# Twelve weight chunks per layer through GpSimd DMAs, from four pairs of buffers, in a two-layer streaming encoder

## The chip, the cores and the metric

The kernel runs on one core of one Trainium2 chip. The metric is the device time of one execution in microseconds; lower is better. The engines are called PE (TensorE), PEld (its weight load), DVE (VectorE), ACT (ScalarE), POOL (GpSimd) and SP (SyncE, which here only issues DMAs).

## The reference

A sequence of 512 positions of width 1024 passes through two layers. Each layer is a half-step SwiGLU feed-forward block, a mixer, and a second half-step feed-forward block, all with RMS norm and a shift, a scale and a gate that come from a vector c. All data and weights are float32. The mixer, cut to what matters here:

```python
proj = h @ w_in                       # q, k, v of branch A; u of B; q, k, v of C; forget logits; gates
ya = chunked_relpos_attention(qa, ka, va, ..., rel_bias)          # 8 heads of 64, own chunk and 8 before
yb = multiscale_pool(ub, w_pool, pool_scale)
yc = forgetting_attention(qc, kc, vc, ..., f_lin + forget_bias)   # 8 heads of 64, causal, decaying bias
branch = einsum('bsnw,nwd->bsnd', stack([ya, yb, yc]), w_branch)
merged = sum(sigmoid(g_lin) * branch, over the 3 branches)
return merged @ w_out
```

## The kernel before

**Products.** A float32 weight or activation is held as two parts of the format fp32r: a high part (`hi`) and the remainder (`lo`). `triple` forms each product from three matmuls: hi x hi (L119), lo x hi (L120, here the weight's low part, written `acc<-wlo,hhi`) and hi x lo (L121). `hhi` and `hlo` are the two parts of the normed activations.

**Weight chunks.** `wchunk` (L237 to 265) fetches 512 KB of float32 weights by a DMA that SP issues into a tile of the tag `raw`, which has two buffers (`NRAW` = 2). ACT casts it to the high part `whi` (L262), and `lo_eng` subtracts that from the raw values to give `wlo` (L264). `whi` and `wlo` have three buffers each. `lo_eng` is DVE, except between the start of the attention of branch A and the end of that of branch C, where `LO_SHARE` = 1 gives every subtraction to POOL.

**The stage around the change.** The weights of q, k, v of branch A are columns 0, 1, 2 of `w_qkv`, those of branch C columns 3, 4, 5; each column is four chunks. `proj` streams chunks 0 and 1 of a column past all four row tiles; chunks 2 and 3 are `held`, and used row tile by row tile, so that each row tile is finished in turn. `Mixer.run` first drains columns 0 to 2. Then `attention(..., "a")` runs the eight heads of branch A, and between its steps takes matmuls from a filler: `fill_a` is columns 3, 4, 5 and then the forget gates (`forget`). The attention of branch C follows, with the gates and branch products (`merge_units`, from weight chunks `w_branch` and `w_ubg`) as its filler. In the profile, the filler's columns of layer 0 run from 471 to 576 us, those of layer 1 from 1716 to 1821 us.

**The order.** Program order gives each tile and its buffer; `later` and `poll` place the transposes and value products of a head among the filler's matmuls by a count of PE work (`pe`). A tile scheduler then lays each engine's instructions in one fixed order. An engine takes its queue strictly in that order, and waits at an instruction whose inputs or whose target buffer are not ready; a DMA waits in the queue of the engine that issues it.

**Steps of the attention that come up later.** L765 and L766: logits (two matmuls). L769: bias and maximum on DVE. L773: exponential on ACT. L776: division by the row sum, as a `tensor_scalar` on DVE. L788: transposes on PE. L792 and L793: high and low part of the transposed probabilities (`pta`, `ptb`), on ACT and DVE. L810 and L811: value products. L814, L815, L369, L370: output of a head and its split. L270 to L278: Newton steps for the inverse norms of q and k (`nt_v`, `nt_j`, `nt_q`, `nt_u`, `nt_z`) on DVE; L653: their application, on DVE and POOL. L712, L713, L716: forget logits. L196, `v<-in_w_ada_dram`: the weight loads of the modulation, elsewhere in the program.

Of the kernel before, what the change touches and what calls it, by code (L numbers as in the profile page):

```python
# [22 lines left out]
P = 128  # L23
T = 512
# [16 lines left out]
def encoder_kernel(tc, xT, c, w_ada, b_ada, gains, w_gate, w_up, w_down, w_qkv, w_f, w_ubg,  # L41
# [22 lines left out]
    def st(shape, dt, tag, bufs):  # L64
        return sb.tile(shape, dt, tag=tag, bufs=bufs, name=nm(tag))
# [171 lines left out]
    def wchunk(src, shape, side=True, spare=None, lo_eng=None):  # L237
        if lo_eng is None:
            lo_share[1] += 1
            lo_eng = nc.gpsimd if lo_share[0] and lo_share[1] % lo_share[0] == 0 else nc.vector  # L240
        if quiet[0] > 0:
            quiet[0] -= 1
            if quiet[0] == 0:
                gate.clear()
        elif side and in_ffn[0] and mod_tag[0] == "v2":
            mod_credit[0] += MOD_RATE
            while mod_credit[0] >= 1.0:
                mod_credit[0] -= 1.0
                mod_pop()
        raw = st([P] + list(shape), F32, "raw", NRAW)  # L250
        last["dma"] = nc.sync.dma_start(raw, src).ins
        if spare == "ptb":
            both = st([P, 2] + list(shape), F32R, "ptb", 2)
            hi, lo = both[:, 0], both[:, 1]
        elif spare == "b":
            hi = st([P] + list(shape), F32R, "b", NB)
            lo = st([P] + list(shape), F32R, "b", NB)
        else:
            hi = st([P] + list(shape), F32R, "whi", 3)
            lo = st([P] + list(shape), F32R, "wlo", 3)  # L260
        with behind("scalar"):
            nc.scalar.copy(hi, raw)  # L262
        with behind("vector"):
            lo_eng.tensor_tensor(lo, raw, hi.bitcast(F32), op=ALU.subtract)  # L264
        return hi, lo


    def rsqrt(v, n):
# [307 lines left out]
            return [self.act(n, *pgs[n]) for n in range(3)]  # L576


    def qkv_chunk(l, col, c, **kw):
        return wchunk(w_qkv[l, 2 * c * P:(2 * c + 2) * P, col * T:(col + 1) * T]  # L580
                      .rearrange("(k p) c -> p k c", p=P), (2, T), **kw)

    def proj(l, col, evac, pre=None, norm=None):
        accs = [acc() for _ in range(NT)]

        def three(t, k, hi, lo):
            tk = slice(t * P, (t + 1) * P)
            triple2(accs[t], hhi[:, k, tk], hlo[:, k, tk], hi, lo, k == 0, k == KD - 1)

        if norm is not None:  # L590
            for hs in range(2):
                norm.back(hs, mmt)
                if hs == 0:
                    later(FRONT2, lambda: norm.front(1, mmt))
                    later(BACK2, lambda: norm.back(1, mmt))
                for k in range(6):
                    hi, lo = pre[k // 2]
                    for t in (2 * hs, 2 * hs + 1):
                        three(t, k, hi[:, k % 2, :], lo[:, k % 2, :])
        else:  # L600
            for c in range(2):
                hi, lo = qkv_chunk(l, col, c)
                for kk in range(2):
                    for t in range(NT):
                        three(t, 2 * c + kk, hi[:, kk, :], lo[:, kk, :])
                        yield
        held = [(c, *qkv_chunk(l, col, c)) for c in ((3,) if pre else (2, 3))]
        for t in range(NT):
            for c, hi, lo in held:
                for kk in range(2):  # L610
                    three(t, 2 * c + kk, hi[:, kk, :], lo[:, kk, :])
                    yield
            evac(t, accs[t])
# [1 line left out]
    def triple2(o, lh, ll, rh, rl, start, stop):  # L615
        triple(o, lh, ll, rh, rl, start, stop)

    def proj_v(l, col, tag, res):
        vt = [None] * NT

        def evac(t, a):
            b = st([P, H, 2, HD], F32R, tag, 4)
            a3 = a.rearrange("p (h d) -> p h d", h=H)
            for odd in range(2):
                hi, lo = b[:, odd::2, odd, :], b[:, odd::2, 1 - odd, :]
                split_to(hi, lo, a3[:, odd::2, :])
            vt[t] = b

        yield from proj(l, col, evac)
        res.extend(vt)  # L630

    def proj_qk(l, col, gcol, is_q, res, pre=None, norm=None):
# [70 lines left out]
    def forget(l):  # L703
        raw = st([P, KD, H], F32, "wf", 1)
        nc.sync.dma_start(raw, w_f[l])
        f2 = st([P, KD, 40], F32R, "ssum", 1)
        nc.gpsimd.memset(f2.bitcast(F32), 0.0)
        split_to(f2[:, :, :H], f2[:, :, 32:32 + H], raw)
        pf = mmt()
        for k in range(KD):  # L710
            poll()
            mm(pf[:40, :], f2[:, k, :], hhi[:, k, :], start=(k == 0), stop=False)  # L712
            mm(pf[:40, :], f2[:, k, :], hlo[:, k, :], start=False, stop=(k == KD - 1))  # L713
            pe[0] += 2.0
        z = t1(T)[:H, :]
        nc.scalar.copy(z, pf[32:32 + H, :])  # L716
# [196 lines left out]
    def drain(*gens):  # L913
        for it in gens:
            for _ in it:
                pass

    class Mixer:
# [10 lines left out]
        def run(self, nxt):  # L929
            l = self.l  # L930
            in_ffn[0] = False
            for b in range(4):
# [2 lines left out]
            g8 = qg8[:, l, :]  # L935
            qa, ka, va, qc, kc, vc = [], [], [], [], [], []
            ya, yb, yc = [], [], []
            drain(proj_qk(l, 0, g8[:, 0:1], True, qa, self.pre, self.norm),
                  proj_qk(l, 1, g[:, 1:2], False, ka), proj_v(l, 2, "xv", va))
            finish_turns()  # L940
            turns.clear()
            heads[0] = 0

            def fill_a():
                yield from proj_qk(l, 3, g8[:, 2:3], True, qc)
                yield from proj_qk(l, 4, g[:, 3:4], False, kc)
                yield from proj_v(l, 5, "v2", vc)
                yield from forget(l)

            lo_share[0] = LO_SHARE  # L950
# [134 lines left out]
```

## Time and profile before

| what | value |
|---|---|
| three runs | 2504.58, 2512.98, 2509.06 us |
| median | 2509.06 us |
| the profiled execution, its own time | 2514.29 us |
| its span in the profile | 2512.5 us |
| granted PE clock, mean over the span | 0.995 |
| weight chunks through `wchunk` | 395 casts on ACT, of which 24 are the change's |

The span is what the hardware profiler recorded from the first to the last instruction; every row below is from that one execution. In a row of a timeline the columns are start, duration, engine, line, operation and output<-inputs; the square bracket at its end is the engine's idle time before it and what ended that. A row of groups gives count, busy time, mean in ns, then the idle time before the group's instructions. In a row on DMA issues the last figure is the median time from issue to landing.

### The profile page before, as it was taken

The numbers are of one execution on the slowest core, as the hardware profiler recorded it, in microseconds if no ns is written. First come the engines' busy times: TensorE is split into PE (matmuls) and PEld (weight loads), VectorE is DVE, ScalarE is ACT, GpSimd is POOL, SyncE is SP. The second block draws the span as 40 slices with busy tenths as digits, with TensorE's granted clock in tenths as the row PEclk, the third lists the DMA queues.
The fourth block names the chain that finished last, engine by engine and source line by source line (L and its number), as shares of the span: only waits on it lengthen the run. The fifth ranks groups of instructions, "written<-read, shape, count | busy, mean of one in ns | idle before, by whom it ended". The sixth has DMA issues, their size and how long they took to land. (4 is left out here: it accounts for less than half of the span.)

```text
span 2512.5 us, 30820 instructions
## 1 busy us (share of the span) xinstructions
PE 2440.8 (97%) x11898; PEld 2039.0 (81%) x11898; DVE 1374.1 (55%) x2429; ACT 979.7 (39%) x1632; POOL 384.8 (15%) x369
## 2 busy tenths in 40 slices
PE   6999999999999999999999999999899999999999
PEld 5888888777788888888888888877778888888888
DVE  8655536688753365555365543367787434533332
ACT  4322235767532343222332223355766334422231
POOL 2000003243322220000020000123332322100000
PEclk9999999999999999999999999999999999999999
DMA  7655533222323335555335532323233233222322
GB/s 252 227 188 198 191 111 110 76 80 91 107 89 109 119 113 196 185 201 184 101 117 187 192 121 97 118 84 93 64 110 102 92 116 121 74 95 98 97 96 93
DMA packets 116263, 320.02 MB, mean 127 GB/s; under 512 B 11122, under 2 KB 13298, under 8 KB 116116
## 3 DMA queue, kind: packets, MB, share of 16 engines
q1 hardware_dynamic: 116114, 318.05, 37.6%
q8 instruction: 93, 1.52, 0.2%
q14 instruction: 54, 0.44, 0.1%
q10 hardware_dynamic: 2, 0.00, 0.0%
HBM read 311.64 MB, written 6.38 MB: 127 GB/s over the span
## 5 line engine op out<-in xcount | busy, mean ns | idle before, releaser
L262 ACT CAST whi<-raw 128x1024 fp32r<-128x1024 f32 (+1 forms) x395 | 411.7, 1045 | 1096.9 <-PE acc L120 421.5
L264 DVE TENSOR_TENSOR wlo<-raw,whi 128x1024 fp32r<-128x1024 f32 x339 | 419.0, 1238 | 532.2 <-ACT whi L262 520.1
L120 PE MATMUL mm<-hlo,whi 128*128 128x512 f32 x1304 | 507.8, 389 | 0.0
L121 PE MATMUL mm<-hhi,wlo 128*128 128x512 f32 x1304 | 507.7, 389 | 0.0
L119 PE MATMUL mm<-hhi,whi 128*128 128x512 f32 x1304 | 507.6, 389 | 0.0
L119 PE MATMUL acc<-b,whi 128*128 128x512 f32 (+1 forms) x960 | 359.0, 374 | 0.0
L121 PE MATMUL acc<-b,wlo 128*128 128x512 f32 (+1 forms) x960 | 357.2, 372 | 0.0
L120 PE MATMUL acc<-b,whi 128*128 128x512 f32 (+1 forms) x960 | 356.6, 372 | 0.0
L121 PEld LDWEIGHTS mm<-hhi,wlo 128*128 128x128 f32 x1304 | 245.0, 188 | 51.0
L119 PEld LDWEIGHTS mm<-hhi,whi 128*128 128x128 f32 x1304 | 245.0, 188 | 51.0
L120 PEld LDWEIGHTS mm<-hlo,whi 128*128 128x128 f32 x1304 | 245.0, 188 | 50.7
L309 POOL TENSOR_TENSOR ssum<-ssum,t 128x256 f32<-128x256 f32 (+1 forms) x45 | 53.6, 1190 | 1082.4 <-ACT t L308 1082.4
L121 PEld LDWEIGHTS acc<-b,wlo 128*128 128x128 f32 x960 | 184.6, 192 | 29.8
L120 PEld LDWEIGHTS acc<-b,whi 128*128 128x128 f32 x960 | 184.5, 192 | 29.1 <-DVE b L370 0.3
L119 PEld LDWEIGHTS acc<-b,whi 128*128 128x128 f32 x960 | 184.6, 192 | 28.9
L196 DVE CUSTOM_DVE_ANT_0 v<-v,b,badac 128x1024 f32<-128x1024 f32 x144 | 183.8, 1279 | 35.5 <-DMA v<-in_w_ada_dram 35.4
L119 PE MATMUL acc<-hhi,whi 128*128 128x512 f32 x480 | 192.0, 401 | 3.2 <-ACT hhi L555 3.2
L121 PE MATMUL acc<-hhi,wlo 128*128 128x512 f32 x480 | 190.1, 396 | 3.3 <-POOL wlo L264 3.1
L120 PE MATMUL acc<-hlo,whi 128*128 128x512 f32 x480 | 189.4, 395 | 1.5 <-DVE hlo L557 1.5
L454 DVE TENSOR_TENSOR t<-mm,t 128x512 f32<-128x512 f32 x86 | 59.4, 691 | 212.7 <-PE mm L121 208.6
L264 POOL TENSOR_TENSOR wlo<-raw,whi 128x1024 fp32r<-128x1024 f32 (+1 forms) x56 | 133.6, 2389 | 175.3 <-ACT whi L262 145.8
L119 PE MATMUL acc<-whi,hhi 128*128 128x512 f32 x336 | 138.2, 411 | 4.9 <-ACT t L642 3.7
(233 smaller groups left out, 3552.9 us busy)
## 6 DMA issues: line engine op xcount, KB each, us to landing
v<-in_w_ada_dram SPq DMA_DIRECT2D x144, 512.0 KB, 4.4
raw<-in_w_down_dram SPq DMA_DIRECT2D x88, 512.0 KB, 3.7
raw<-in_w_gate_dram SPq DMA_DIRECT2D x85, 512.0 KB, 3.4
raw<-in_w_up_dram SPq DMA_DIRECT2D x85, 512.0 KB, 3.4
raw<-in_w_ubg_dram SPq DMA_DIRECT2D x56, 512.0 KB, 3.5
raw<-in_w_qkv_dram SPq DMA_DIRECT2D x48, 512.0 KB, 3.7
raw<-in_w_branch_dram SPq DMA_DIRECT2D x24, 512.0 KB, 3.7
raw<-in_w_out_dram SPq DMA_DIRECT2D x16, 512.0 KB, 3.7
```

The source lines that it names most:

```text
L119: mm(o, lh, rh, start=start, stop=False)
L120: mm(o, lh, rl, start=False, stop=False)
L121: mm(o, ll, rh, start=False, stop=stop)
L196: nc.vector.tensor_tensor_reduce(out=raw, in0=raw, in1=silc[0], scale=1.0, scalar=badac[:, l, j, d:d + 1], op0=ALU.mult, op1=ALU.add, accu ...
L262: nc.scalar.copy(hi, raw)
L264: lo_eng.tensor_tensor(lo, raw, hi.bitcast(F32), op=ALU.subtract)
L309: nc.gpsimd.tensor_tensor(self.ssum[:, cols], self.ssum[:, cols], q, op=ALU.add)
L454: nc.vector.tensor_tensor(pr, pu, sg, op=ALU.mult)
```

## The change

The 12 chunks of columns 3, 4 and 5 no longer go through `wchunk`. A `Stream` makes both parts of each: `begin` lets a DMA issued by GpSimd convert the float32 weights to fp32r on their way into `hi`; `end` lets ACT write the negated high part into `lo` and a second DMA of GpSimd add the same weights of the DRAM onto it, which leaves the remainder. `get`, called where a chunk is wanted, begins chunks up to two ahead (`AHEAD` = 2) and ends them up to one ahead. Chunk 0 is begun and ended while column 2 is being computed (`early`, called behind the request of that column's held chunks). Every fourth chunk takes the two `raw` buffers as its pair, so that there are four pairs with the three of `whi` and `wlo`. The matmuls are the same.

```diff
+    class Stream:
+        AHEAD = 2
...
+        def early(self):
+            self.begin()
+            self.end()
+
+        def begin(self):
+            n = self.begun
+            self.begun += 1
+            if n % 4 == 3:
+                hi, lo = (st([P] + self.shape, F32R, "raw", NRAW) for _ in range(2))
+            else:
+                hi, lo = st([P] + self.shape, F32R, "whi", 3), st([P] + self.shape, F32R, "wlo", 3)
+            nc.gpsimd.dma_start(hi, self.chunks[n])
+            self.parts.append((hi, lo))
+
+        def end(self):
+            hi, lo = self.parts[self.ended]
+            nc.scalar.activation(lo, hi.bitcast(F32), AF.Copy, scale=-1.0)
+            nc.gpsimd.dma_start(lo, self.chunks[self.ended], accum_op=ALU.add)
+            self.ended += 1
+
+        def get(self):
+            n = self.at
+            self.at += 1
+            while self.begun < len(self.chunks) and self.begun <= n + self.AHEAD:
+                self.begin()
+            while self.ended < self.begun and self.ended <= n + 1:
+                self.end()
+            return self.parts[n]
...
     def qkv_chunk(l, col, c, **kw):
-        return wchunk(w_qkv[l, 2 * c * P:(2 * c + 2) * P, col * T:(col + 1) * T]
-                      .rearrange("(k p) c -> p k c", p=P), (2, T), **kw)
+        if stream[0] is not None:
+            return stream[0].get()
+        return wchunk(qkv_src(l, col, c), (2, T), **kw)
...
         held = [(c, *qkv_chunk(l, col, c)) for c in ((3,) if pre else (2, 3))]
+        if held_hook is not None:
+            held_hook()
...
+            coming = Stream([qkv_src(l, col, c) for col in (3, 4, 5) for c in range(4)], [2, T])
             drain(proj_qk(l, 0, g8[:, 0:1], True, qa, self.pre, self.norm),
-                  proj_qk(l, 1, g[:, 1:2], False, ka), proj_v(l, 2, "xv", va))
+                  proj_qk(l, 1, g[:, 1:2], False, ka), proj_v(l, 2, "xv", va, coming.early))
...
             def fill_a():
+                stream[0] = coming
                 yield from proj_qk(l, 3, g8[:, 2:3], True, qc)
                 yield from proj_qk(l, 4, g[:, 3:4], False, kc)
                 yield from proj_v(l, 5, "v2", vc)
+                stream[0] = None
                 yield from forget(l)
```

In the changed file the new class is L267 to 304: the high part's DMA is L288, the negation L293, the accumulating DMA L294. What stood at L653 stands at L700 there, L739 is L786, L765 and L766 are L812 and L813, L788 is L835. In the fences that follow, a number behind a tile's name tells the tiles of one tag apart.

POOL's queue in layer 0, at the start of the stage, before (`ptb` is the k of branch A being normalised):

```order
L653 TENSOR_TENSOR ptb_528_3228<-ptb_528_3228,nt_z_553_3345 128x512 x2
L264 TENSOR_TENSOR wlo_595_3559<-raw_593_3556,whi_594_3558 128x1024
L264 TENSOR_TENSOR wlo_612_3618<-raw_610_3615,whi_611_3617 128x1024
L264 TENSOR_TENSOR wlo_634_3698<-raw_632_3695,whi_633_3697 128x1024
L264 TENSOR_TENSOR wlo_637_3704<-raw_635_3701,whi_636_3703 128x1024
L740 MEMSET strip_671_3850 64x64
```

And after. Chunk 0 is `whi_570` and `wlo_571`, chunk 1 `whi_595` and `wlo_596`, chunk 2 `whi_597` and `wlo_598`, chunk 3 the pair of raw buffers, `raw_613` (high) and `raw_614` (low):

```order
L288 DMA raw_613_3622<-in_w_qkv_dram 128x2x512
L700 TENSOR_TENSOR ptb_528_3228<-ptb_528_3228,nt_z_553_3345 128x512 x2
L288 DMA whi_570_3429<-in_w_qkv_dram 128x2x512
L294 DMA raw_614_3623<-in_w_qkv_dram 128x2x512
L294 DMA wlo_571_3430<-in_w_qkv_dram 128x2x512
L288 DMA whi_595_3561<-in_w_qkv_dram 128x2x512
L288 DMA whi_597_3564<-in_w_qkv_dram 128x2x512
L294 DMA wlo_596_3562<-in_w_qkv_dram 128x2x512
L294 DMA wlo_598_3565<-in_w_qkv_dram 128x2x512
L288 DMA whi_634_3701<-in_w_qkv_dram 128x2x512
```

In place of each subtraction two DMAs now stand in POOL's queue, and chunk 3 goes ahead of chunk 0.

PE's queue where chunk 1 is first used, before (row tile by row tile, three matmuls each):

```order
L766 MATMUL mm_604_3603<-b_571_3440,b_527_3213 128x384
L119 MATMUL acc_589_3552<-whi_611_3617,hhi_114 128x512
L120 MATMUL acc_589_3552<-wlo_612_3618,hhi_114 128x512
L121 MATMUL acc_589_3552<-whi_611_3617,hlo_115 128x512
L119 MATMUL acc_590_3553<-whi_611_3617,hhi_114 128x512
L120 MATMUL acc_590_3553<-wlo_612_3618,hhi_114 128x512
```

After, in layer 0:

```order
L813 MATMUL mm_607_3610<-b_573_3445,b_527_3213 128x384
L119 MATMUL acc_591_3557<-whi_595_3561,hhi_114 128x512
L119 MATMUL acc_592_3558<-whi_595_3561,hhi_114 128x512
L119 MATMUL acc_593_3559<-whi_595_3561,hhi_114 128x512
L119 MATMUL acc_594_3560<-whi_595_3561,hhi_114 128x512
L835 MATMUL mm_615_3639<-ident_66,t2_602_3587 128x128 x2
L812 MATMUL mm_616_3644<-b_573_3445,b_526_3212 128x512
L120 MATMUL acc_591_3557<-wlo_596_3562,hhi_114 128x512
L121 MATMUL acc_591_3557<-whi_595_3561,hlo_115 128x512
```

Four L119, the transposes and a logit product now stand ahead of the first L120, which reads chunk 1's low part. Elsewhere in the stage PE's order is the one of before.

SP's queue at the end of the stage of layer 0, before:

```order
L251 DMA raw_862_4514<-in_w_qkv_dram 128x2x512
L251 DMA raw_971_4886<-in_w_branch_dram 128x2x512
L739 DMA strip_891_4631<-in_rel_dram 128x512
L251 DMA raw_974_4892<-in_w_ubg_dram 128x1024
L251 DMA raw_1016_5058<-in_w_ubg_dram 128x1024
L251 DMA raw_1074_5264<-in_w_branch_dram 128x2x512
```

And after:

```order
L786 DMA strip_839_4451<-in_rel_dram 128x512
L786 DMA strip_879_4619<-in_rel_dram 128x512
L251 DMA raw_959_4874<-in_w_branch_dram 128x2x512
L251 DMA raw_962_4880<-in_w_ubg_dram 128x1024
L251 DMA raw_1004_5046<-in_w_ubg_dram 128x1024
L251 DMA raw_1062_5252<-in_w_branch_dram 128x2x512
```

The column's loads are gone from SP. The first two loads of the next stage, `raw_959` and `raw_962`, take the two buffers that chunk 11, the last of the stream and again a fourth one, has filled with its high and low part.

More of the change, by code (lines that the diff above doesn't have):

```diff
@@ L265, in wchunk, with __init__ @@
         return hi, lo
+    class Stream:
+        AHEAD = 2
+        def __init__(self, chunks, shape):
+            self.chunks, self.shape = chunks, shape
+            self.begun, self.ended, self.at = 0, 0, 0
+            self.parts = []
+        def early(self):
[23 more added lines that the diff above has]
+            return self.parts[n]
     def rsqrt(v, n):
@@ L576, in start, with qkv_src, proj @@
             return [self.act(n, *pgs[n]) for n in range(3)]
+    stream = [None]
+    def qkv_src(l, col, c):
+        return w_qkv[l, 2 * c * P:(2 * c + 2) * P, col * T:(col + 1) * T].rearrange("(k p) c -> p k c", p=P)
     def qkv_chunk(l, col, c, **kw):
-        return wchunk(w_qkv[l, 2 * c * P:(2 * c + 2) * P, col * T:(col + 1) * T]
-                      .rearrange("(k p) c -> p k c", p=P), (2, T), **kw)
-    def proj(l, col, evac, pre=None, norm=None):
+        if stream[0] is not None:
+            return stream[0].get()
+        return wchunk(qkv_src(l, col, c), (2, T), **kw)
+    def proj(l, col, evac, pre=None, norm=None, held_hook=None):
         accs = [acc() for _ in range(NT)]
@@ L616, in triple2, with proj_v @@
         triple(o, lh, ll, rh, rl, start, stop)
-    def proj_v(l, col, tag, res):
+    def proj_v(l, col, tag, res, held_hook=None):
         vt = [None] * NT
@@ L627, in evac @@
             vt[t] = b
-        yield from proj(l, col, evac)
+        yield from proj(l, col, evac, held_hook=held_hook)
         res.extend(vt)
```

## The prediction

> **What bounds the kernel now.** I read the page's busy table first, then a table of the two stages that the change touches, then PE's waits in them.
>
> ```profile
> span 2512.5 us, 30820 instructions
> PE 2440.8 (97%) x11898; PEld 2039.0 (81%) x11898; DVE 1374.1 (55%) x2429; ACT 979.7 (39%) x1632; POOL 384.8 (15%) x369
> ```
>
> PE is busy 97% of the span, and the change neither adds nor removes a matmul. So time can move only through PE's waits and its clock. In the stretch of columns 3 to 5 (layer 0, then layer 1; the columns are length, then busy time and count of PE, PE's loads, DVE, ACT, POOL, then clock, DMA share and rate):
>
> ```profile
> 471.00:576.00 105.00, 98.19 (x504) 79.37 (x503) 80.53 (x209) 72.41 (x160) 40.91 (x30) 0.98 0.24 73
> 1716.00:1821.00 105.00, 96.64 (x504) 77.97 (x503) 80.69 (x209) 72.45 (x160) 41.29 (x30) 1.00 0.24 73
> ```
>
> PE lacks 6.8 us of the 105 in layer 0 and 8.4 us in layer 1. DVE at 77% is the next engine; ACT stands at 69%, POOL at 39%, the DMA engines at 24%. What PE waits for, from 471 to 590 us (total, times, longest):
>
> ```profile
> PE mm L765 <- DVE t L815: 1.6, 2, 1.1
> PE mm L788 <- DVE nt_z L278: 1.2, 1, 1.2
> ...
> PE mm L811 <- DVE ptb L793: 0.8, 1, 0.8
> ...
> PE mm L810 <- ACT pta L792: 0.2, 1, 0.2
> ```
>
> Twelve rows, 7.6 us together, nearly all on DVE, and not one names a weight part (whi or wlo) or its DMA: the weights are on time now. Whatever the change does for their transport brings nothing by itself. It can bring time only by freeing DVE, and it can cost time by making a weight late.
>
> **What goes.** Per layer the change removes 12 casts on ACT, 12 subtractions on POOL and 12 loads of SP:
>
> ```profile
> L264 POOL TENSOR_TENSOR wlo<-raw,whi 128x1024 fp32r<-128x1024 f32 x14 | 33.7, 2412 | 56.1 <-ACT whi L262 43.0 <-PE acc L119 8.8 <-issue 4.2
> L262 ACT CAST whi<-raw 128x1024 fp32r<-128x1024 f32 x15 | 15.7, 1049 | 2.2 <-PE acc L121 2.0
> L653 POOL TENSOR_TENSOR ptb<-ptb,nt_z 128x512 f32<-128x512 f32 x4 | 6.0, 1518 | 7.3 <-DVE nt_z L278 7.3
> raw<-in_w_qkv_dram SPq DMA_DIRECT2D x9, 512.0 KB, 3.6
> ```
>
> Off POOL go 12 x 2.41 = 28.9 us. On ACT a negation of the same shape stands for each cast; I price it at the cast's 1.05 us, so nothing changes there in sum. Why POOL's passes matter:
>
> ```profile
> 542.12 4.76 POOL L264 TENSOR_TENSOR wlo<-raw,whi 128x1024 fp32r<-128x1024 f32 x2 [8.85 <-PE acc L119]
> 544.60 2.32 DVE L270 TENSOR_SCALAR nt_j<-nt_v 128x32 int32<-128x32 int32 x1
> 506.01 0.18 DVE L270 TENSOR_SCALAR nt_j<-nt_v 128x32 int32<-128x32 int32 x1
> 541.19 0.28 DVE L776 TENSOR_SCALAR t<-t,rs 128x128 f32<-128x128 f32 x1
> 487.40 2.03 DVE L776 TENSOR_SCALAR t<-t,rs 128x128 f32<-128x128 f32 x1
> ```
>
> The same small DVE operation lasts 0.18 us alone and 2.32 us when it meets a POOL subtraction; the one of L776 0.28 and 2.03 us. It holds DVE for about as long as POOL's pass lasts. The page "SBUF — State Buffer" of the Trainium skill (section "Who interferes with whom") describes this as an exclusive lock on a port that DVE and GpSimd share, and the rows above agree.
>
> This block at 544.60 ends in a PE wait, and in something worse:
>
> ```profile
> 547.84 0.52 PE L788 MATMUL mm<-ident,t 128*128 128x128 f32 x3 [1.21 <-DVE nt_z L278]
> 545.00:549.00 4.00, 2.52 (x13) 1.51 (x11) 3.87 (x10) 0.69 (x2) 1.88 (x1) 1.00 0.62 177
> 549.00:553.00 4.00, 4.00 (x13) 3.39 (x14) 3.83 (x11) 2.32 (x5) 2.05 (x2) 0.57 0.43 151
> 1798.93 0.66 PE L788 MATMUL mm<-ident,t 128*128 128x128 f32 x4 [1.70 <-DVE t L776]
> 503.62 2.36 DVE L648 TENSOR_SCALAR nt_v<-qss 128x32 f32<-128x32 f32 x1
> 507.30 0.39 PE L811 MATMUL mm<-ptb,xv 128*128 128x256 f32 x1 [0.83 <-DVE ptb L793]
> 548.99 0.44 PE L811 MATMUL mm<-pta,xv 128*128 128x256 f32 x1 [0.23 <-DVE pta L793]
> ```
>
> After the 1.21 us gap the granted clock falls from 1.00 to a mean of 0.57 over four us: (1 - 0.57) x 4 = 1.7 us of work lost. Layer 1 has its gap at the same place (1.70 us) without such a fall.
>
> Gain, layer 0: the waits of 1.2 and 0.8 us (the second at 507.3, with a blocked operation of DVE 1.3 us ahead of it), 0.2 for the short one at 548.99, and 1.7 of clock: 3.9 us. Layer 1: 1.2 + 0.8 + 0.2 and the 1.7 of 1798.93: 3.9 us. The rest of the waits, 5.4 us in layer 0, is the attention's own chain through DVE, which I leave in place. From below, the gain is 0 if the GpSimd DMAs hold DVE as the passes did; from above it is all 7.6 us plus 1.7.
>
> **What comes: the start.** Chunk 0 is prepared early. Chunk 1 is not: its pair takes buffers that column 2's held chunks leave.
>
> ```profile
> 469.74 0.39 PE L121 MATMUL acc<-whi,hlo 128*128 128x512 f32 x1
> 475.35 0.19 ACT L773 ACTIVATION_READ_ACCUMULATOR t<-t,mx 128x1 f32 x1
> 478.53 0.39 PE L119 MATMUL acc<-whi,hhi 128*128 128x512 f32 x1
> v<-in_w_ada_dram SPq DMA_DIRECT2D x144, 512.0 KB, 4.4
> 544.55 0.37 SPq L251 DMA_DIRECT2D raw<-in_w_qkv_dram  x1
> ```
>
> The first buffer is free at 469.74 + 0.39 = 470.1. I know no duration for a GpSimd issue here. It lies between SP's 0.37 us for the same bytes and POOL's full pass of 2.41; nearer to the first, since issuing touches no data: 1.0 us. The plain load I give the slower of the landings shown, 4.4 us: hi 1 is there at 475.5. Its negation stands on ACT right behind the first exponential, which ends at 475.54, and lasts to 476.6. Only then can the accumulating DMA be issued: 476.6 + 1.0, and a landing. An accumulating transfer has no row; it cannot beat the plain 3.6 us and, if it reads as well as writes its target, I bound it by twice 4.4 us. I take 5.0, near the lower end, since DMA is at 24%. So lo 1 lands at 482.6. PE needs hi 1 at 478.53 and, since the new order issues four L119s first (4 x 0.23 us from start to start), two transposes and a logit product ahead of the first L120, lo 1 at about 480.0. Stall: **2.6 us**. Bounds: 0.4 of issue and 3.6 give 480.6, so 0.6; 2.4 of issue twice with 4.4 and 8.8 give 470.1 + 6.8 + 1.05 + 11.2 = 489.2, so 9 us.
>
> The page "DMA: Bandwidth & Descriptors" of the Trainium skill (section "Anatomy of one DMA — SWDGE (gpsimd) path") gives about 2.0 us plus the bytes over 436 GB/s, an estimate of 3.2 us for 512 KB. By it the stall would be nothing, and my total 5 us lower; the rows here hold no GpSimd DMA of weights, so none can show it yet.
>
> **The end.** Chunk 11 is the fourth pair's, that is, it fills both raw buffers until PE has used it. The next two raw loads (branch weights, then gate weights) now wait for that; before, they were issued at 546.91 and, the last of them, 562.19.
>
> ```profile
> 546.91 0.37 SPq L251 DMA_DIRECT2D raw<-in_w_branch_dram  x1
> 562.19 0.33 SPq L251 DMA_DIRECT2D raw<-in_w_ubg_dram  x1
> raw<-in_w_ubg_dram SPq DMA_DIRECT2D x56, 512.0 KB, 3.5
> 575.41 0.40 PE L121 MATMUL acc<-whi,hlo 128*128 128x512 f32 x1
> 579.83 0.58 ACT L716 COPY t<-mm 8x512 f32<-8x512 f32 x1 [0.80 <-PE mm L713]
> 581.26 0.44 PE L119 MATMUL acc<-hhi,whi 128*128 128x512 f32 x1
> 582.21 0.40 PE L121 MATMUL acc<-hhi,wlo 128*128 128x512 f32 x1
> ```
>
> Both buffers are free at 575.8. SP issues (0.33 and 0.37), the two land at about 579.6 and 579.8, ACT casts the branch chunk to 580.65, copies (0.58) and casts the gate chunk to 582.3. POOL, still the engine for these subtractions, makes the branch's low part by 583.05 and the gate's by 585.45. PE wants the gate's parts at 581.26 and 582.21: it waits 1.0, then 2.2 more, **3.2 us**. DVE cannot hide that, nor other PE work, whose order here is fixed. The low bound is 0.8 us (POOL takes the gate chunk first), the high 5 us with landings of 4.4.
>
> **Clock and the middle.** A gap of 1.2 us cost a half-clock stretch once in layer 0 and a gap of 1.70 none in layer 1. With two gaps of 2.6 and 3.2 us per layer I count one more stretch: **1.7 us** (0 to 3.4). In the middle, chunks 4 to 11 are begun two ahead. A negation waits on ACT, in order, until its high part has landed, and the exponentials and evacuations stand behind it; the accumulating DMA waits on POOL for the negation, with the next load and the normalisation of ptb (1.5 us each) behind it. A chunk's share of the stage is 105 / 12 = 8.75 us; two landings, a negation and two issues take 1.0 + 4.4 + 1.05 + 1.0 + 5.0 = 12.4 us, within the two chunks, 17.5 us, that it is begun ahead. So PE should not wait for weights, but ACT idles here and there: **1.0 us** (0 to 24: up to 3 us at each of eight chunks, if both landings are 8.8). SP loses 12 issues that it had time for: nothing.
>
> Per layer 2.6 + 3.2 + 1.7 + 1.0 - 3.9 = +4.6, for two layers +9.2 us. The profiled run took 2514.29 us, and 2523.5 would be its counterpart; against the median of 2509.06 I forecast **2518.3 us**.
>
> **Rivals.**
> First, DVE's relief wins (faster). If a GpSimd DMA does not hold DVE and lands like SP's, the start costs 0.6, the end 0.8 to 1, the clock nothing, and the gain reaches 7.6: about -6 per layer, -12 in all, 2497. It decides from the point where the start's and end's stalls together stay under 3.9 us. For it speaks the 2.03 for 0.28 us above; against it, that the raw buffers are held to the last matmul, which no speed of a DMA changes.
> Second, the GpSimd DMAs are slow (slower): the start costs 9, and the eight later chunks up to 3 us each, less a gain of 0: +36 per layer. At half of that, +36 in all: 2545. For it speaks that DVE is busy 77% of the stage, and that the issuing engine shares something with it that makes one wait for the other for 2 us. The page "SBUF — State Buffer" (section "SBUF: two separate sides") says that DVE's two-port operations keep GpSimd from writing DMA descriptors, and that the wait lengthens a DMA from 620 to 3100 ns; the rows show the lock only between two computing engines.
> Third, everything is covered and what is gained is given back: within 3 us of before, 2509.
>
> **Chances.** 0.3%, 7.5 us, is about what a measurement here can tell from no change. My forecast's own range is +2 to +20 us, chance 0.46, of which 0.29 lies beyond 7.5. DVE's relief 0.23 (0.20 faster by more than the bound), slow DMAs 0.18, all slower, everything covered 0.13. Together faster 0.20, same 0.33, slower 0.47. The range runs from 2500 (most of the first rival) to 2547 (half of the second).
>
> **What would show it.** Right: PE waits on wlo near 480 and 1725, on whi and wlo of the gate near 581 and 1826, with the raw loads issued just after 575.8; L270 and L776 back at 0.2 to 0.3 us until there. Wrong: landings of the accumulating DMA far from 5 us, a DVE operation stretched beside a GpSimd issue, or waits on weights in the middle of the stage.

## The result: 1.0% slower

The changed kernel takes 2533.14 us (median of four runs, 2530.06 to 2539.72), the kernel before 2507.51 us (median of four, with one more run): ratio 1.0103, 95% interval 1.0075 to 1.0131, or about 25.6 us. The forecast was 2518 us, in a range of 2500 to 2547. The profiled execution of the changed kernel took 2530.06 us:

```profile
span 2528.3 us, 30839 instructions
PE 2442.9 (97%) x11898; PEld 2038.8 (81%) x11898; DVE 1367.0 (54%) x2429; ACT 979.1 (39%) x1632; POOL 374.4 (15%) x393
```

PE, DVE and ACT have the same instructions as before; POOL has 24 more, for 48 DMAs in place of 24 subtractions. The two stretches of columns 3 to 5, between the same clock times as before:

```profile
471.00:576.00 105.00, 93.60 (x483) 76.00 (x482) 69.74 (x202) 67.85 (x153) 27.96 (x35) 0.98 0.53 110
1716.00:1821.00 105.00, 92.95 (x466) 74.99 (x465) 67.69 (x193) 66.64 (x147) 29.44 (x37) 0.97 0.56 117
```

Each engine does less in them than before, PE too (93.60 of 105 us for 98.19): no engine has become the bound, they wait for each other. The share of the DMA engines went from 0.24 to 0.53. PE's waits from 468 to 600 us:

```profile
PE acc L120 <- DMA wlo<-in_w_qkv_dram: 2.9, 1, 2.9
PE acc L121 <- POOL wlo L264: 2.7, 1, 2.7
PE mm L812 <- DVE pta L840: 2.6, 1, 2.6
PE mm L812 <- DVE b L720: 2.2, 1, 2.2
PE mm L835 <- DVE t L823: 1.3, 2, 1.2
...
PE acc L119 <- ACT whi L262: 0.7, 1, 0.7
```

Two waits on low parts are new, one at each end of the stage, and two on DVE are longer than any before. Where the time goes is best seen by taking the same matmul in both traces and subtracting its starts:

| matmul | layer 0: before, after | shift | layer 1: before, after | shift |
|---|---|---|---|---|
| near the stage's start | 471.11, 468.62 | -2.5 | 1715.55, 1718.09 | +2.5 |
| after chunk 1 began | 484.62, 485.24 | +0.6 | 1729.51, 1738.00 | +8.5 |
| last of chunk 11 | 575.41, 577.04 | +1.6 | 1820.03, 1829.74 | +9.7 |
| after the gate's first chunks | 604.58, 612.50 | +7.9 | 1851.20, 1866.65 | +15.5 |

So the start costs 3.1 and 6.0 us, the middle 1.0 and 1.2, the end 6.3 and 5.8: 10.4 + 13.0 = 23.4 us, near the 25.6 of the medians. The two profiled spans are only 15.8 us apart. The rest lies outside these stages, where nothing was changed: in three places (389, 1263 and 1635 us) the execution before has half-clock stretches of 3.4 us, 1.7 us of work each, that the one after hasn't, 5 us in all; the rest of it was not followed up. The first of the three, before and then after (the clock is the third figure from the right):

```profile
388.00:392.00 4.00, 3.65 (x18) 3.65 (x19) 2.56 (x14) 0.17 (x1) 0.00 (x0) 0.59 0.44 132
```

```profile
388.00:392.00 4.00, 4.00 (x33) 3.95 (x34) 3.14 (x15) 0.85 (x3) 0.36 (x1) 1.00 0.27 103
```

### The profile page after: what moved, and what is told of

The parts are those of the page before. It is cut to its first block, busy times and chain, and to the rows that moved or that the text cites. A ratio compares the mean times of both kernels' runs of the same rounds, so it can differ in the third digit from the quotient of the medians.

```text
span 2528.3 us, 30839 instructions
## 1 busy us (share of the span) xinstructions
PE 2442.9 (97%) x11898; PEld 2038.8 (81%) x11898; DVE 1367.0 (54%) x2429; ACT 979.1 (39%) x1632; POOL 374.4 (15%) x393
## 5 line engine op out<-in xcount | busy, mean ns | idle before, releaser
L262 ACT CAST whi<-raw 128x1024 fp32r<-128x1024 f32 (+1 forms) x371 | 386.8, 1046 | 1092.1 <-PE acc L120 417.0
L120 PE MATMUL mm<-hlo,whi 128*128 128x512 f32 x1304 | 507.7, 389 | 0.0
L119 PE MATMUL mm<-hhi,whi 128*128 128x512 f32 x1304 | 507.6, 389 | 0.0
L119 PE MATMUL acc<-b,whi 128*128 128x512 f32 (+1 forms) x960 | 356.4, 372 | 0.0
L120 PE MATMUL acc<-b,whi 128*128 128x512 f32 (+1 forms) x960 | 354.9, 370 | 0.0
L120 PEld LDWEIGHTS mm<-hlo,whi 128*128 128x128 f32 x1304 | 245.1, 188 | 50.9
L119 PEld LDWEIGHTS mm<-hhi,whi 128*128 128x128 f32 x1304 | 245.1, 188 | 50.8
L120 PEld LDWEIGHTS acc<-b,whi 128*128 128x128 f32 x960 | 182.3, 190 | 29.6 <-DVE b L409 0.8
L119 PEld LDWEIGHTS acc<-b,whi 128*128 128x128 f32 x960 | 182.1, 190 | 29.0
L119 PE MATMUL acc<-hhi,whi 128*128 128x512 f32 x480 | 192.1, 401 | 4.6 <-ACT hhi L594 3.2
L120 PE MATMUL acc<-hlo,whi 128*128 128x512 f32 x480 | 190.9, 398 | 1.5 <-DVE hlo L596 1.5
L119 PE MATMUL acc<-whi,hhi 128*128 128x512 f32 x288 | 117.5, 411 | 6.7 <-ACT t L689 4.7
L120 PE MATMUL acc<-wlo,hhi 128*128 128x512 f32 x288 | 115.2, 400 | 5.8 <-DMA wlo<-in_w_qkv_dram 5.7
```

What stands on the lines that cost most here:

```text
L119: mm(o, lh, rh, start=start, stop=False)
L120: mm(o, lh, rl, start=False, stop=False)
```

## The experiments

All of them are compared with runs of the kernel before on the same chip. "Shift" means the table's subtraction. Where a run is set against the changed kernel, or against another experiment, the two did not always run together; the medians of the kernel before range from 2506.3 to 2509.3 us, so such a difference is good to 2 or 3 us.

**What POOL's passes cost.** In the kernel before, the 12 chunks' subtraction is left out:

```diff
+        if no_lo[0]:                     # set while columns 3 to 5 are made
+            return hi, hi
         with behind("vector"):
             lo_eng.tensor_tensor(lo, raw, hi.bitcast(F32), op=ALU.subtract)
```

> The kernel before, with POOL's subtraction left out for the 12 chunks of each layer: the low part's matmuls read the high part instead, so the values are not the reference's. It shows by itself what POOL's passes cost. Theory (they hold DVE, and 3.9 us per layer of PE's time hang on that): 8 us less than before, 2500 us. Rival (the attention's chain through DVE has slack, or waits elsewhere): within 3 us of before.

2498.51 us against 2509.33 (ratio 0.9955, 0.9941 to 0.9969): 10.8 us, 5.4 per layer. What POOL's passes take from DVE does cost PE time, somewhat more than the 3.9 us that I had counted. The rival falls.

**The end.** Chunk 11 gets a pair of its own, so that the raw buffers are free when the gate's loads are due:

```diff
-            if n % 4 == 3:
+            if n in (3, 7):
```

> Chunk 11 takes a whi and a wlo buffer instead of the two raw buffers; chunks 3 and 7 still take the raw pair. Theory (the raw pair held to the end costs time at the end of the stage): the branch and gate loads are issued early again, PE's waits of 0.7 and 2.7 us on the gate's parts go, and with the half-clock stretch behind them the end gives back the 6.5 (layer 0) and 6.0 us (layer 1) by which it shifted PE: about 12 us less than the changed kernel, 2521 us. Rival (the GpSimd DMAs are slow throughout, and the end only shows a delay that would come out elsewhere): less than 4 us gained, 2529 or more.

2526.34 us (ratio to before 1.0066, 1.0052 to 1.0079), 7 us less than the changed kernel (8.6 by the two distances to the kernel before), where 12 were expected. The loads now go out at 548.3 and 548.8 us and PE's waits on the gate's parts are gone: in the shift the end adds nothing any more (10.7 us at 581 and at 600). But the 10.7 us were lost by then: start (5.7 us, with a half-clock stretch at 485) and middle (4.7) cost more than in the changed kernel (3.1 and 1.0). The theory was right on the end, and had nothing on why the middle moves.

**The start.** Chunk 1 takes the raw pair instead of chunk 3:

```diff
-            if n % 4 == 3:
+            if n in (1, 7, 11):
```

> Chunk 1 takes the raw pair (with chunks 7 and 11), so that both its parts can be made before the stage begins; the end stays as changed. Theory (chunk 1's chain of load, negation and accumulation is late by 2.9 us): PE's wait on wlo at the start goes, and with it 3.1 us in layer 0 and about 6 in layer 1, where a half-clock stretch followed: 2524 us. Rival (the next GpSimd DMA in the queue is late in its place, chunk 2 or 3): no gain, 2531 to 2535 us, with a new wait on a low part within 15 us.

2535.28 us (1.0101, 1.0086 to 1.0116): no gain, as the rival had it, though not by its mechanism. At 485 us the shift against 476 is nil, so chunk 1 no longer stalls PE; by 500 us six microseconds are lost again, and on another wait: PE's transposes wait for DVE's `t`, 1.44 and 2.56 us, not for a low part. Something between these engines is late.

**Both.** The raw pair for chunks 1, 5 and 9:

```diff
-            if n % 4 == 3:
+            if n in (1, 5, 9):
```

> The raw pair goes to chunks 1, 5 and 9, so that start and end are both mended. Theory: the two gains add, about 21 us less than the changed kernel, 2512 us, and what is left against the kernel before is the middle, about +1 us per layer. Rival (waits move on): the gains do not add, 2520 us or more.

2523.57 us (1.0057, 1.0043 to 1.0071), 9.6 us less than the changed kernel and not 21. Start and end are mended, as the shift says (-2.1 at 470 us, -0.9 at 485; 7.1 at 575, 7.1 at 600); all that is lost is lost between 485 and 520 us (from -0.9 to 9.4). What stands there on ACT:

```profile
480.85 0.37 ACT L839 CAST pta<-mm 128x256 fp32r<-128x256 f32 x1 [1.55 <-PE mm L835]
485.70 1.06 ACT L293 ACTIVATE wlo<-whi 128x1024 fp32r<-128x1024 f32 x1 [4.48 <-DMA whi<-in_w_qkv_dram]
486.67 0.70 ACT L820 ACTIVATE t<-t,mx 128x512 f32<-128x512 f32 x1
...
495.72 1.06 ACT L293 ACTIVATE raw<-raw 128x1024 fp32r<-128x1024 f32 x1 [5.30 <-DMA raw<-in_w_qkv_dram]
496.68 0.57 ACT L687 COPY ptb<-acc 128x512 f32<-128x512 f32 x1
497.14 0.51 ACT L820 ACTIVATE t<-t,mx 128x256 f32<-128x256 f32 x1
```

ACT sits 4.48 and 5.30 us at a negation whose high part hasn't landed, and the next exponential stands behind it. DVE then divides by that exponential's sum, and PE transposes the quotient:

```profile
488.24 0.66 PE L835 MATMUL mm<-ident,t 128*128 128x128 f32 x4 [1.10 <-DVE t L823]
498.43 0.44 PE L835 MATMUL mm<-ident,t 128*128 128x128 f32 x2 [3.09 <-DVE t L823]
```

PE's wait names DVE, and DVE is not the cause of these two: two engines back is a DMA. In the changed kernel the same happens in smaller steps, 2.72 us at 493 and 2.31 us at 509:

```profile
493.15 1.06 ACT L293 ACTIVATE wlo<-whi 128x1024 fp32r<-128x1024 f32 x1 [2.72 <-DMA whi<-in_w_qkv_dram]
509.11 1.06 ACT L293 ACTIVATE raw<-raw 128x1024 fp32r<-128x1024 f32 x1 [2.31 <-DMA raw<-in_w_qkv_dram]
```

They are not equally dear. PE's shift grows by 0.6 us from 485 to 500, past the first of them, and the second is followed by the longest wait of the middle, 2.63 us, and a half-clock stretch from 516.3. On its way to that wait stands something else, too:

```profile
510.69 0.17 DVE L822 RECIPROCAL rs<-sm 128x1 f32<-128x1 f32 x1 [1.67 <-ACT t L820]
511.25 2.52 POOL L700 TENSOR_TENSOR ptb<-ptb,nt_z 128x512 f32<-128x512 f32 x2
511.28 3.65 DVE L700 TENSOR_TENSOR ptb<-ptb,nt_z 128x512 f32<-128x512 f32 x2
515.19 0.49 PE L812 MATMUL mm<-b,b 128*128 128x512 f32 x1 [2.63 <-DVE pta L840]
```

```profile
509.11 2.14 DVE L653 TENSOR_TENSOR ptb<-ptb,nt_z 128x512 f32<-128x512 f32 x2
```

DVE waits 1.67 us for the late exponential, divides, and comes to its half of the normalisation 0.03 us after POOL has begun the other half: the first of its two operations lasts 3.05 us. In the kernel before (the last row) DVE came first, and the two last 2.14 us together. So some 1.5 us of the wait come from the meeting with POOL that the delay brought about. Layer 1 has the same 3.65 us at 1763.97 and the wait of 2.64 us behind it.

Why these two high parts come too late for ACT is seen in POOL's queue. Chunk 5's DMA stands there behind chunk 4's accumulating one, which waits for ACT's negation; chunk 7's stands behind a memset that waits for another load:

```profile
485.65 1.19 POOL L294 DMA_DIRECT2D wlo<-in_w_qkv_dram  x1 [7.99 <-ACT wlo L293]
486.39 1.21 POOL L288 DMA_DIRECT2D whi<-in_w_qkv_dram  x1
504.54 0.14 POOL L787 MEMSET strip<- 64x64 f32 x1 [4.36 <-DMA strip<-in_rel_dram]
505.00 0.73 POOL L288 DMA_DIRECT2D raw<-in_w_qkv_dram  x1 [0.31 <-PE mm L813]
```

The last matmul on chunk 1, whose buffers chunk 5 takes, ends at 482.6, the last on chunk 3, whose pair chunk 7 takes, at 502.0. The two DMAs go out 3.8 and 3.0 us after that and land in 6.7 and 4.1 us; ACT goes on when they have landed. So ACT and POOL hand their waits to each other. An estimate from these rows: begun at 502.0 and landed 4.1 us later, chunk 7's high part is there at 506.1, before ACT is done with the step ahead of its negation (506.8), and the dearer of the two waits is gone.

**Taking that wait away.** Two runs from the kernel just above. In one the negation reads other data of the same shape, which is there before the stage begins; in the other there is neither negation nor accumulation:

```diff
-            nc.scalar.activation(lo, hi.bitcast(F32), AF.Copy, scale=-1.0)
+            nc.scalar.activation(lo, hhi[:, 0:2, :].bitcast(F32), AF.Copy, scale=-1.0)
```

> As the kernel with the raw pair for chunks 1, 5 and 9 (2523.6 us), with every instruction and every DMA kept, but the negation on ACT reads the normed activations instead of the chunk's high part, so that it waits for no landing (the values are not the reference's). Theory (ACT waits in its queue at a negation for the high part's landing, 1 to 5 us each, with exponentials behind it, and DVE and PE's transposes after those): ACT's waits on DMAs go, and 15 to 25 us with them: 2500 to 2508 us. Rival (the accumulating DMAs, or ACT's and POOL's load, cost the time): 2518 or more.

2500.43 us against 2508.69 (0.9973, 0.9963 to 0.9983): 23.1 us less than with the wait, with the same count of instructions and DMAs. ACT no longer waits at any of the 12 for a high part, and POOL's accumulating DMAs no longer wait for it either. The order is not the same: without that dependence the scheduler places the negations, and some steps of DVE and POOL, elsewhere, and DVE comes ahead of POOL at the normalisation again (2.14 us). So the 23 us are the price of the dependence with the order that follows from it, not of the waiting alone.

```diff
             hi, lo = self.parts[self.ended]
-            nc.scalar.activation(lo, hi.bitcast(F32), AF.Copy, scale=-1.0)
-            nc.gpsimd.dma_start(lo, self.chunks[self.ended], accum_op=ALU.add)
+            self.parts[self.ended] = (hi, hi)
```

> As the kernel with the raw pair for chunks 1, 5 and 9 (2523.6 us), but each chunk is only its high part: the DMA of GpSimd that converts stays, the negation on ACT and the accumulating DMA are left out, and the matmuls of the low part read the high part (the values are not the reference's). Theory (neither the GpSimd issues nor the transfers cost PE time; the negation's place on ACT does): as fast as the kernel before without POOL's subtractions, 2498 us, within 4. Rival (GpSimd's DMAs hold DVE or land too late by themselves): 2508 or more.

2491.62 us (0.9937, 0.9921 to 0.9952): 17 us faster than before, 6 more than I gave it. ACT's casts are gone here as well as POOL's subtractions, and I had counted only the latter; that the casts make up the 6 us was not tested. The GpSimd DMAs that convert cost PE nothing that can be seen: none of its waits names one. Negation and accumulation together cost 8.8 us even where the negation doesn't wait (2500.43 - 2491.62); which of the two was not measured apart.

**The same on the changed kernel itself**, with its own pairs:

> The changed kernel as it is (the raw pair for chunks 3, 7 and 11), with only the negation reading the normed activations in place of the high part, so that ACT waits for no landing (the values are not the reference's). Theory (three costs: chunk 1's chain, ACT's waits in the middle, the raw pair at the end): the middle goes, and the start becomes shorter since the accumulation need not follow the high part's landing, but the end's 6.5 and 6.0 us stay: 2508 to 2516 us, with PE's wait on the gate's low part as before. Rival (the negation's wait is the whole loss, and the end is only its echo): 2500 to 2504.

2512.06 us (1.001, 1.000 to 1.002), 21 us less than the changed kernel. The stage's parts by the shift: start +1.9 and +2.3 us, middle -5.6 and -5.4, end +6.3 and +6.5. PE's wait at the end is unchanged, 0.8 us on the high part and 2.7 on the low one:

```profile
580.78 0.80 PE L121 MATMUL acc<-hhi,wlo 128*128 128x512 f32 x1 [2.67 <-POOL wlo L264]
```

So the end is a cost of its own, and no echo. The program of this run and that of 2500.43 us differ in nothing but the chunks that take the raw pair, and the two lie 12 us apart by their distances to the kernel before: the same 6 us per layer. The middle is 6.6 us per layer better than in the changed kernel (1.0 and 1.2 to -5.6 and -5.4). That is the price of the negation's dependence there, again with the order that goes with it (chunk 7's DMA now stands ahead of that memset and goes out at 501.33), and -5.5 is what the middle gains without it, close to the 5.4 per layer of the run without subtractions. The traces show most of what the 6.6 us consist of in layer 0: the wait of 2.63 us at 515, gone here; the half-clock stretch behind it, 1.7 us; and 1.3 us at a wait that has no DMA in it. Changed kernel and this run:

```profile
540.66 0.30 PE L812 MATMUL mm<-b,b 128*128 128x128 f32 x1 [2.18 <-DVE b L720]
```

```profile
533.95 0.30 PE L812 MATMUL mm<-b,b 128*128 128x128 f32 x1 [0.86 <-DVE b L720]
```

The kernel before waits 0.86 us here too. In the changed kernel an exponential stands on ACT ahead of the steps (L714, L717) whose results this wait is for, and two L119 that PE did ahead of the wait in the kernel before now stand behind it. PE's order thus differs in a second place from the one of before. This part is order; no run here changes that order and nothing else.

**Half of the change.** The kernel before, in which ACT's cast is followed by ACT's negation and a GpSimd DMA adds the weights:

```diff
+        if by_dma[0]:                    # set while columns 3 to 5 are made
+            nc.scalar.activation(lo, hi.bitcast(F32), AF.Copy, scale=-1.0)
+            nc.gpsimd.dma_start(lo, src, accum_op=ALU.add)
+            return hi, lo
```

> The kernel before with one half of the change: SP's load and ACT's cast make the high part as before, then ACT writes its negative into the low part and a GpSimd DMA adds the weights onto it; POOL's subtraction goes. The negation never waits for a DMA of its own, since it reads what ACT has just written; ACT has 12 passes of 1.05 us more per layer. Theory (the wait at the negation is what costs, not the accumulating DMA): faster than before, 2500 to 2506 us. Rival (the low part lands too late, cast, negation and accumulation in a row, or ACT's 12.6 us more per layer delay the exponentials): 2512 or more.

2513.91 us (1.0021, 1.0009 to 1.0033), 5 us slower than before, and the rival's: the low part is late. PE waits for it three times in layer 0, and half-clock stretches follow at 480 and 552 us:

```profile
PE acc L120 <- DMA wlo<-in_w_qkv_dram: 4.4, 3, 2.4
```

**A later negation.** From the kernel with pairs 1, 5 and 9: chunk 1 is prepared with chunk 0, and a negation is queued behind the second exponential after its chunk was begun.

```diff
+        def after_exp(self, ins):        # called behind each exponential
...
+            while self.ended < self.begun and self.seen[self.ended] >= 2:
+                self.end()               # negation queued behind ins
```

> The kernel with the raw pair for chunks 1, 5 and 9, with chunk 1 prepared early as chunk 0 is, and each later negation queued on ACT behind the second exponential after its chunk was begun (or the last one before the chunk is wanted), and each high part's DMA behind the accumulating one of two chunks before. The result is the full one. Theory (the negation stands too early on ACT): most of ACT's waits on DMAs go, PE waits on low parts stay under 3 us per layer: 2500 to 2510 us. Rival (put later, the negation makes the low part late for PE instead): PE waits on wlo in the middle of the stage, 2518 or more.

2534.47 us (1.011, 1.0092 to 1.0128): the theory falls as I had put it. ACT's waits at negations are down from 13.3 us in layer 0 to 1.4, and PE pays instead:

```profile
PE acc L120 <- DMA wlo<-in_w_qkv_dram: 12.9, 7, 4.0
```

The wait is ACT's if the negation stands early, PE's if it stands late. This run changes two things at once, since each high part's DMA also stands behind the accumulating one of two chunks before; which of them makes the low parts late it doesn't tell.

**More lead.** A chunk is begun as soon as its pair is used up, three ahead where no held chunk is in the way:

```diff
-            while self.begun < len(self.chunks) and self.begun <= n + self.AHEAD:
+            while self.begun < len(self.chunks) and (self.begun < 4 or self.begun - 4 < self.used):
                 self.begin()
```

> The late negations of the run before, with a longer lead: a chunk is begun as soon as the pair it takes has been used up in the program's order (three ahead, except past two held chunks), and its negation stands behind the first (chunks 2 and 3) or second exponential after that, and ahead of the request two chunks on. Raw pair for chunks 1, 5 and 9; the result is the full one. Theory (a chunk needs its high part's landing, the negation and the accumulation's landing, about 5 + 1 + 1.2 + 6 = 13 us, and with 17.5 us or more of lead neither ACT nor PE has to wait): 2500 to 2510 us. Rival (the lead that four pairs can give doesn't suffice, since column by column two pairs are held): PE still waits 5 us or more on low parts per layer, 2515 or more.

2516.49 us against 2506.30 (1.0040, 1.0026 to 1.0054): 10 us slower than before where the short lead was 26 slower. The time is the rival's; its sign, PE waits of 5 us or more on low parts, is not there. What was left were single negations: 1.86 us of ACT's time at chunk 4, 3.55 at chunk 8, and PE waits on `wlo` of 3.4 us. Each negation was then put by the landings that this trace showed:

```diff
-            while ... self.seen[self.ended] >= (1 if self.ended < 4 else 2):
+            while ... self.seen[self.ended] >= (1, 1, 1, 1, 3, 2, 1, 1, 4, 2, 1, 1)[self.ended]:
```

> The kernel with the longer lead (2516.5 us against 2506.3 for the one before), with the negation of each chunk put where its trace showed the high part landed: behind the first exponential after its start for chunks 2, 3, 6, 7, 10 and 11, the second for 5 and 9, the third for 4 and the fourth for 8. The result is the full one. Theory (what is left are ACT's waits of 1.9 and 3.6 us at chunks 4 and 8 and PE's 3.4 us on low parts, with the half-clock stretches behind them): 2504 to 2512 us. Rival (moving one negation only shifts the wait to the next): 2514 to 2520.

2506.35 us against 2507.99 (0.9993, 0.9982 to 1.0003): 27 us faster than the changed kernel and no different from the one before. The theory held. This is the fastest version here that leaves nothing out; it gives back all that the change cost, and wins nothing that can be measured.

**The negation on POOL**, directly ahead of its accumulating DMA:

```diff
-            nc.scalar.activation(lo, hi.bitcast(F32), AF.Copy, scale=-1.0)
+            nc.gpsimd.tensor_scalar(lo, hi.bitcast(F32), -1.0, None, op0=ALU.mult)
```

> The kernel with the raw pair for chunks 1, 5 and 9 (2523.6 us), with the negation on POOL in place of ACT, directly ahead of the accumulating DMA; the result is the full one. ACT then has no instruction that waits for a landing; POOL has 12 passes per layer again, with one input. Theory (the wait in ACT's queue is the cost): ACT's waits on DMAs go; if the passes hold DVE as the subtractions did, the kernel comes out like the one before, 2505 to 2512 us, if they don't, near 2500. Rival (the wait matters wherever it stands, since low parts come late): 2518 or more, with PE waits on wlo.

2535.85 us (1.012, 1.0105 to 1.0134), as the rival had it, with a PE wait of 3.8 us on a low part. ACT's waits at negations are gone and the time is longer: the wait now holds POOL's queue, where the normalisation of `ptb` stands behind it, and a DVE operation held by the pass takes 3.32 us:

```profile
L293 POOL TENSOR_SCALAR wlo<-whi 128x1024 fp32r<-128x1024 f32 x9 | 26.5, 2942 | 24.9 <-DMA whi<-in_w_qkv_dram 22.2 <-issue 2.7
PE mm L705 <- POOL ptb L700: 6.0, 2, 5.7
518.91 3.32 DVE L823 TENSOR_SCALAR t<-t,rs 128x512 f32<-128x512 f32 x1
```

## Why the prediction was right, and where its sum was short

The direction, the places and the range held; the predicted loss, 9.2 us, was well short of 25.6. The range of 2500 to 2547 us took in a gain as well as a loss, so the time alone says little; the terms say more. Step by step, per layer:

| term | forecast | layer 0, layer 1 |
|---|---|---|
| start, with its clock | 2.6 | 3.1, 6.0 |
| end, with its clock | 3.2 + 1.7 | 6.3, 5.8 |
| ACT's waits in the middle, with clock and order | 1.0 | 6.6, 6.6 |
| DVE's relief (the middle without those waits) | -3.9 | -5.6, -5.4 |

**The start was right in size and mechanism.** The negation stood behind the first exponential, the accumulating DMA behind the negation, and PE waited 2.93 us where I had 2.6:

```profile
472.91 1.04 ACT L293 ACTIVATE wlo<-whi 128x1024 fp32r<-128x1024 f32 x1
474.26 1.22 POOL L294 DMA_DIRECT2D wlo<-in_w_qkv_dram  x1 [4.21 <-ACT wlo L293]
480.48 0.50 PE L120 MATMUL acc<-wlo,hhi 128*128 128x512 f32 x1 [2.93 <-DMA wlo<-in_w_qkv_dram]
```

The two guesses in it were near: a GpSimd issue occupies POOL for 0.9 us (converting) or 1.21 (accumulating), where I took 1.0; the landings, counted from the start of the issue, are 4.7 and 6.1 us, where I took 1.0 and 4.4, and 1.0 and 5.0:

```profile
L294 POOL DMA_DIRECT2D wlo<-in_w_qkv_dram x9 | 10.9, 1211 | 38.2 <-ACT wlo L293 33.8 <-PE mm L835 4.2 <-issue 0.2
L288 POOL DMA_DIRECT2D whi<-in_w_qkv_dram x9 | 8.1, 898 | 10.3 <-PE acc L121 9.6 <-PE mm L813 0.6
```

```profile
whi<-in_w_qkv_dram POOLq DMA_DIRECT2D x18, 512.0 KB, 4.7
wlo<-in_w_qkv_dram POOLq DMA_DIRECT2D x18, 512.0 KB, 6.1
```

By the formula that I quoted from the Trainium skill ("DMA: Bandwidth & Descriptors", "Anatomy of one DMA — SWDGE (gpsimd) path") both would be 3.2 us, by that estimate, and the stall nothing. The trace doesn't agree, the accumulating transfer least.

**The end was right to the row.** The loads went out at 577.27 and 577.82, with chunk 11's last matmul, the casts followed, and POOL made the branch's low part ahead of the gate's:

```profile
577.27 0.38 SPq L251 DMA_DIRECT2D raw<-in_w_branch_dram  x1
582.62 1.04 ACT L262 CAST whi<-raw 128x1024 fp32r<-128x1024 f32 x1
582.20 5.12 POOL L264 TENSOR_TENSOR wlo<-raw,whi 128x1024 fp32r<-128x1024 f32 x2 [25.62 <-ACT whi L262]
587.37 0.50 PE L121 MATMUL acc<-hhi,wlo 128*128 128x512 f32 x1 [2.68 <-POOL wlo L264]
```

PE waits 0.69 + 2.68 = 3.4 us for 3.2.

**The gain was right in its mechanism, and 1.5 us short.** DVE's small operation that took 2.32 us is back at 0.18, and the PE waits of 1.2 and 0.8 us behind it are gone:

```profile
548.51 0.18 DVE L309 TENSOR_SCALAR nt_j<-nt_v 128x32 int32<-128x32 int32 x1
```

The GpSimd issues do not hold DVE in any way that its operations show here: 89 of them run beside such an issue and no other POOL work, and none is more than 0.11 us over the median of its kind. The rule of the Trainium skill's page "SBUF — State Buffer" (section "SBUF: two separate sides") that DVE holds up GpSimd's descriptors, up to 3100 ns, does not show in the issues either: their mean stays at 0.9 and 1.21 us while DVE is busy two thirds of the time. Whether a part of the landings, 3.9 to 7.8 us, is such a wait these rows do not tell.

**The step that failed** is the middle: "PE should not wait for weights, but ACT idles here and there: 1.0 us". The first half held; the second was mis-sized at 1.0 for 6.6 us. I had added up the chain of landings (12.4 us) against the 17.5 us of lead and concluded that it fits, which is a statement on PE. The same sum says nothing on the engine in the chain's midst: ACT reaches the negation in its fixed order, ahead of the landing, and hands its wait to the exponentials. And the sum takes it that a chunk is begun as soon as its buffers are free, where POOL's queue let chunks 5 and 7 start 3.8 and 3.0 us later. ACT's two waits are 5.0 us in layer 0; with the meeting of DVE and POOL and the half-clock stretch behind the second, and the changed order at 540, PE pays 6.6. The bound of 24 us held the value; the choice near its low end had no row behind it. None of the signs of being wrong that I had named looks at ACT: the accumulating DMA landed about when I had it, no DVE operation was stretched beside an issue, and PE waited for no weight in the middle.

**The clock.** One reading of mine was wrong: layer 1's gap at the place of the 1.21 us is 1.18 us, at 1792.48, and the one of 1.70 us comes 6.5 us later. The clock stayed at 1.00 behind both of them, so the choice of one stretch per layer is as open as before. I counted one more half-clock stretch per layer, and one of before gone in layer 0. From the stage's start to 635 us there are three after against two before, and in layer 1's stage three against none. Equal gaps differ: the start's stall was followed by a granted clock of 1.00 in layer 0 and 0.57 in layer 1.

```profile
480.00:484.00 4.00, 3.52 (x16) 2.93 (x17) 0.70 (x2) 0.43 (x1) 0.00 (x0) 1.00 1.01 240
1731.00:1735.00 4.00, 3.58 (x9) 2.87 (x10) 0.00 (x0) 0.00 (x0) 0.00 (x0) 0.57 1.03 245
```

That explains why the start costs about 3 us more in layer 1, with a wait on DVE's `xv` that is 0.9 us longer there; why the one gap lowers the clock and the other doesn't, these runs do not settle.

## What to carry to other kernels

When a transfer is put between two steps of a chain, ask which engine carries the step behind it: an engine with a fixed order waits there with all its other work, so a chain that is early enough for the last consumer can still cost time through the engine in its midst. Follow a wait back past the engine that the profile names: PE waited for DVE, DVE for ACT, ACT for a landing, and only giving the negation other data to read told that apart from the DMAs' own cost. Such a run can also change the order of the queues; compare the order before its whole difference is put down to the wait. A buffer that is borrowed costs what its owner's next use costs: chunk 11 in the raw pair cost 6 us per layer by itself.

## What the runs showed of the hardware

A POOL pass over one input (`tensor_scalar`, 2.94 us) took longer than the subtraction of two inputs of the same shape (2.41 us), and held DVE as that did. Which of DVE and POOL begins first can matter more than what they do: with DVE 0.04 us ahead its first normalising operation lasts 0.69 us (before, at 509.11), with POOL 0.03 us ahead 3.05 us (changed kernel, at 511.28). An accumulating DMA lands 1.4 us later than a converting one of the same bytes (6.1 for 4.7 us), and a converting one that is issued behind two accumulating ones can take over 7: in the kernel with pairs 1, 5 and 9, chunk 4's was issued at 478.08, and its negation began at 485.70.
